# Layer A's attention on one core: two units' outputs in one PSUM bank, and a third bank for late logits

## The chip, the cores and the metric

The kernel runs on one core of one Trainium2 chip. The metric is the device time of one execution in microseconds (us). The kernel before took 2687.64 us, the median of three runs (2687.32, 2687.64 and 2689.79).

## What is computed

Two pre-norm residual layers over 1024 tokens of width 1024. Layer A is sparse attention (16 query heads of 64, one shared key/value head; an indexer picks 256 keys per token) and a squared-ReLU MLP; layer B is latent attention and another MLP. The part that the change touches is layer A's attention, in blocks of 128 queries:

```python
def block(args):                       # one block of 128 queries
    ...
    logits = jnp.einsum('bqhd,bqkd->bhqk', qb, kg) * (A_HEAD_DIM ** -0.5)
    bias = rel_bias[t5_bucket(idx - t[None, :, None])]
    logits = logits + jnp.transpose(bias, (0, 3, 1, 2))
    logits = jnp.where(valid[:, None], logits, NEG)
    p = jax.nn.softmax(logits, axis=-1)
    return jnp.einsum('bhqk,bqkd->bqhd', p, vg)
```

The kernel does not gather the keys: it computes the logits over all admissible keys and adds a mask (`score`, after selection) that is hugely negative at the keys not picked.

## The kernel before

Everything is float32; for speed a matmul operand is split into a high and a low float32r part (`split_evac`, L88: ScalarE casts the high part out of PSUM, VectorE or GpSimd subtracts it to get the low part), and each product is two or three matmuls. A tile framework allocates the buffers, sets every semaphore and orders the instructions of each engine at build time by its own timeline; the source order is a hint. So a change of buffers can move instructions that it does not name.

`attend_a` runs twice: for the early query blocks 1, 3, 0, 2 (up to 512 keys, `wide` = 512; 205 to 350 us of the profile) and, after the first MLP on those blocks, for the late blocks 7, 4, 5, 6 (640 to 1024 keys, `wide` = 1024; 757 to 972 us). A unit is one block and two heads (G = 2), so each call has 32 units, (7,0) to (6,7) in the late one. Three kinds of step are woven, the logits of unit k beside the values of unit k-1:

- `logits` (L543 to L554), per head: TensorE computes `lps`, 128 queries by up to 512 keys, in one PSUM bank (two banks, one after the other, for over 512 keys); VectorE reads it once, adding bias (`bm`) or mask (`score`) and taking the running minimum of the negative, into `lg` in SBUF (L548); ScalarE takes the exponential and the sum (L552), VectorE the reciprocal (L553), GpSimd scales (L554). Six `lg` buffers are there in the late call.
- `values` (L566 to L572), per two key blocks: TensorE transposes the probabilities of both heads into `ppt`; `ph` and `pl` (two SBUF buffers each) are its split; then four matmuls of 256 columns accumulate into `po`, 128 x 256 in PSUM.
- `output` (L580 to L584): ScalarE copies two quarters of `po` to SBUF (`of`, two copies), and VectorE adds them to the other two quarters of `po` and writes `res` (two adds). The second add, L584, is the last reader of `po`.
- `project` (L1066, in `out_proj`): the output projection `pwoa` of a finished block, spread over the next eight units. The late call spreads its first one from block 4 on.

PSUM has eight banks of 512 float32 columns. The early call gets the logits' four banks from its caller (`lp` is given), and has two for `pt` (transposes), one for `po`, one for `pwo`. The late call opens its own pool of logits banks, `bufs=2`, and has three for `pt`, two for `po` (half of each is used), one for `pwo`.

Of the kernel before, what the change touches and what calls it, by code (L numbers as in the profile page):

```python
# [10 lines left out]
F32 = mybir.dt.float32  # L11
# [7 lines left out]
P = 128  # L19
# [23 lines left out]
class Trunk:  # L43
# [433 lines left out]
    def attend_a(self, tbs, res, kh, kl, vv, score, edge, near_d, wst, lp=None, start=None, beside=None, free=None):  # L477
# [4 lines left out]
        H, G = 16, 2  # L482
        wide = (max(tbs) + 1) * P
        nm0 = f"{tbs[0]}"
        with ExitStack() as st:
            qp = st.enter_context(tc.tile_pool(name="atq" + nm0, bufs=2))
            pp = st.enter_context(tc.tile_pool(name="atp" + nm0, bufs=2, space=PSUM))
            lp = lp or st.enter_context(tc.tile_pool(name="atl" + nm0, bufs=2, space=PSUM))
            queries, probs, outs = {}, {}, {}

            def shape(tb):
                S = (tb + 1) * P
                return S, min(S, 256)
# [5 lines left out]
            def cuts(S, far):  # L499
                if S <= 512:  # L500
                    return [(0, S)]
                cut = min(far, 512)
                return [(0, cut), (cut, S)]
# [17 lines left out]

            def logits(tb, g, i):
                S, nr = shape(tb)
                far = S - nr
                mask = edge[:, 256 - S:256] if tb < 2 else score[tb]
                if i == 0:
                    bm = t2.tile([P, G, 256], F32, name=f"bm{tb}_{g}", tag="bm")
                    src = near_d[G * g:G * g + G, 127:127 + P * 383].rearrange("h (t j) -> t h j", j=383)
                    nc.sync.dma_start(bm[:, :, :nr], src[:, :, 256 - nr:256])
                    nc.gpsimd.tensor_tensor(bm[:, :, :nr], bm[:, :, :nr],  # L530
                                            mask[:, far:].unsqueeze(1).to_broadcast([P, G, nr]), op=ALU.add)
                    small = t2.tile([P, 5 * G], F32, name=f"sm{tb}_{g}", tag="sm")
                    probs[tb, g] = (bm, small, [])
                bm, small, ps_h = probs[tb, g]
                hd = G * g + i
                lg = t2.tile([P, wide], F32, name=f"lg{tb}_{hd}", tag="lg", bufs=6 if wide > 512 else 5)
                mf, mg, mn, sm, rs = (small[:, 5 * i + k:5 * i + k + 1] for k in range(5))

                last = 3.0e38
                for b0, b1 in cuts(S, far):  # L540
                    lps = lp.tile([P, 512], F32, name=f"lps{tb}_{hd}_{b0}", tag="pt")
                    for n, kk in enumerate((kh, kl)):
                        nc.tensor.matmul(lps[:, :b1 - b0], queries[tb][1][:, hd, :], kk[:, b0:b1], start=(n == 0), stop=(n == 1))  # L543
                    for c0, c1 in ((b0, min(b1, far)), (max(b0, far), b1)):
                        if c0 < c1:
                            near = c0 >= far
                            least = mn if near else mg if b0 else mf
                            nc.vector.tensor_tensor_reduce(lg[:, c0:c1], lps[:, c0 - b0:c1 - b0],  # L548
                                                           bm[:, i, c0 - far:c1 - far] if near else mask[:, c0:c1], -1.0, last,
                                                           op0=ALU.add, op1=ALU.min, accum_out=least)  # L550
                            last = least
                nc.scalar.activation(lg[:, :S], lg[:, :S], AF.Exp, bias=mn, scale=-1.0, accum_out=sm)  # L552
                nc.vector.reciprocal(rs, sm)  # L553
                nc.gpsimd.tensor_scalar(lg[:, :S], lg[:, :S], rs, 1.0, op0=ALU.mult, op1=ALU.mult)  # L554
                ps_h.append(lg)

            def values(tb, g, s0):
                nb = tb + 1
                if s0 == 0:
                    outs[tb, g] = pp.tile([P, G * P], F32, name=f"po{tb}_{g}", tag="po", bufs=2 if wide > 512 else 1)  # L560
                po, ps_h = outs[tb, g], probs[tb, g][2]
                ns = min(2, nb - s0)
                pt = pp.tile([P, 2, G, P], F32, name=f"ppt{tb}_{g}_{s0}", tag="pt", bufs=3 if wide > 512 else 2)
                for u in range(ns):
                    for i in range(G):
                        self.anchor = nc.tensor.transpose(pt[:, u, i], ps_h[i][:, (s0 + u) * P:(s0 + u + 1) * P], self.ident)  # L566
                ph = t2.tile([P, 2, G * P], F32R, name=f"ph{tb}_{g}_{s0}", tag="ph")
                pl = t2.tile([P, 2, G * P], F32R, name=f"pl{tb}_{g}_{s0}", tag="pl")
                self.split_evac(ph[:, :ns], pl[:, :ns], pt[:, :ns].rearrange("p u a b -> p u (a b)"))
                for u in range(ns):  # L570
                    for n, m in enumerate((ph, pl)):
                        nc.tensor.matmul(po, vv[:, s0 + u], m[:, u], start=(s0 + u == 0 and n == 0),  # L572
                                         stop=(s0 + u == nb - 1 and n == 1))
# [27 lines left out]
            if beside:  # L601
                spread(beside(lambda shape, name: pp.tile(shape, F32, name=name, tag="pwo", bufs=1)), 0, n0)
# [4 lines left out]
            for k in range(NU + 1):  # L607
                if k == n0 + 1:
                    if free:
                        free()  # L610
                    wop = wst.enter_context(tc.tile_pool(name="awo" + nm0, bufs=1, side="right"))
                    wo, load = self.load_wo(wop, t1, self.d["a_w_o"][0], "a" + nm0)
                    spread(load, n0, n1)
                first = [lambda i=i: logits(*units[k], i) for i in range(G)] if k < NU else []
                second, extra = [], []
                if k:
                    tb, g = units[k - 1]
                    second = [lambda s0=s0: values(tb, g, s0) for s0 in range(0, tb + 1, 2)] + [lambda: output(tb, g)]
                    m = (k - 1 - n1) // each
                    if k > n1 and (k - 1 - n1) % each == 0 and m < 3:  # L620
                        spread(project(tbs[m]), k - 1, k - 1 + each)
                    extra = work[k - 1]
                steps = []
                for i in range(max(len(first), len(second))):
                    steps += second[i:i + 1] + first[i:i + 1]
                weave(steps, extra, self.behind)
# [632 lines left out]
```

## Time and profile before

| | |
|---|---|
| median of three runs | 2687.64 us |
| the profiled execution's own time | 2684.85 us |
| its span, first to last instruction | 2683.0 us |
| mean granted TensorE clock | 0.984 |
| TensorE matmul / weight load busy | 94% / 80% |
| VectorE, ScalarE, GpSimd busy | 57%, 46%, 38% |
| early call, late call | some 145 us and 215 us of the span |

The profiled execution lies 2.79 us under the median of the runs. The shares are means over stages with different limits; the two calls of `attend_a` have far busier VectorE than the MLPs, which fill TensorE alone.

### The profile page before, as it was taken

The page shows a single profiled execution, that of the slowest core. Times are in us where ns is not written, and L with a number is a line of the kernel's source. Part 1 is how long each engine was busy: PE and PEld are TensorE (multiplying, and loading weights), DVE is VectorE, ACT ScalarE, POOL GpSimd, SP SyncE. Part 2 cuts the span into 40 slices and gives each one's busy share as a digit, 9 for nine tenths or more (in the row PEclk, how much of TensorE's full clock was granted, in tenths as well). Part 3 has the DMA queues.
Part 4 walks back from the last instruction along what each step waited for, and adds up shares of the span by engine and source line. Part 5 has one row for each costly group of instructions (what it writes and reads, how often), then busy time and mean ns, then how long its engine had stood idle before and what let it go on. Part 6 is the DMA issues. An engine that isn't in the chain of part 4 may idle for free.

```text
span 2683.0 us, 36853 instructions
## 1 busy us (share of the span) xinstructions
PE 2532.4 (94%) x13354; PEld 2148.5 (80%) x13354; DVE 1521.1 (57%) x3655; ACT 1232.2 (46%) x2989; POOL 1024.1 (38%) x756
## 2 busy tenths in 40 slices
PE   6997799999989999999998999998999999999999
PEld 5897678888768888888888788887778888888887
DVE  5798754999869861222257878897422232222223
ACT  4575744333357764243345777787222222222221
POOL 2235635443556535343324555555121212222120
PEclk9998999999999999999999999999999999999999
DMA  7202323222232223233210000002210101111111
GB/s 157 54 24 60 99 92 97 94 99 90 79 110 68 60 82 127 84 120 106 77 33 11 10 14 10 14 5 80 102 32 32 63 32 63 47 48 48 48 47 63
DMA packets 122293, 173.03 MB, mean 64 GB/s; under 512 B 12752, under 2 KB 101104, under 8 KB 122112
## 3 DMA queue, kind: packets, MB, share of 16 engines
q1 hardware_dynamic: 122112, 170.69, 20.5%
q8 instruction: 105, 1.72, 0.3%
q14 instruction: 76, 0.62, 0.1%
HBM read 159.13 MB, written 11.53 MB: 64 GB/s over the span
## 4 chain that ended last, share of the span: by engine, by line
PE 71%; DVE 7%; DMA 3%; ACT 3%; POOL 2%; issue 2%; SPq 0%; POOLq 0%; DVEq 0%; ACTq 0%
PE pd L1190 25%; PE pu L1120 25%; PE pwo L1066 3%; PE pwoa L1066 2%; PE blps L938 2%; PE bpo L962 2%; PE puq L794 2%; PE po L572 1%; PE ppt L566 1%; PE lps L543 1%; PE pcq L853 1%; PE pukv L750 1%; DVE bpr L939 1%; PE bpt L957 1%; PE pck L853 1%
## 5 line engine op out<-in xcount | busy, mean ns | idle before, releaser
L88 POOL TENSOR_TENSOR dl<-rd,dh 128x1024 fp32r<-128x1024 f32 x96 | 232.4, 2429 | 728.2 <-PE pu L1120 369.3
L1191 DVE TENSOR_TENSOR res<-res,pd 128x1024 f32<-128x1024 f32 x192 | 234.2, 1220 | 419.1 <-PE pd L1190 419.1
L1120 PE MATMUL pu<-mxh,uh 128*128 128x512 f32 (+1 forms) x1056 | 405.4, 384 | 2.4 <-DVE mxl L88 2.4
L1120 PE MATMUL pu<-mxl,uh 128*128 128x512 f32 (+1 forms) x1056 | 404.9, 383 | 0.0
L1120 PE MATMUL pu<-mxh,ul 128*128 128x512 f32 (+1 forms) x1056 | 404.9, 383 | 0.0
L1190 PE MATMUL pd<-dh,hh 128*128 128x512 f32 x1024 | 398.6, 390 | 5.1 <-DVE res L1191 3.1
L1190 PE MATMUL pd<-dl,hh 128*128 128x512 f32 x1024 | 398.5, 389 | 0.0
L1190 PE MATMUL pd<-dh,hl 128*128 128x512 f32 x1024 | 392.9, 389 | 1.6 <-DVE hl L88 1.6
L88 DVE TENSOR_TENSOR hl<-pu,hh 128x512 fp32r<-128x512 f32 (+1 forms) x132 | 88.8, 674 | 407.6 <-ACT hh L88 407.6
L88 ACT CAST dh<-rd 128x1024 fp32r<-128x1024 f32 x96 | 99.1, 1051 | 476.1 <-PE pd L1190 422.5
L88 POOL TENSOR_TENSOR ul<-ru,uh 128x1024 fp32r<-128x1024 f32 x96 | 231.9, 2418 | 167.2 <-ACT uh L88 166.9
L1177 ACT ACTIVATE pu<-pu 128x512 f32<-128x512 f32 (+1 forms) x132 | 75.0, 569 | 433.2 <-PE pu L1120 427.7
L1120 PEld LDWEIGHTS pu<-mxh,uh 128*128 128x128 f32 x1056 | 199.1, 189 | 41.7 <-DVE mxl L88 2.9
L1120 PEld LDWEIGHTS pu<-mxl,uh 128*128 128x128 f32 x1056 | 198.9, 188 | 39.0
L1120 PEld LDWEIGHTS pu<-mxh,ul 128*128 128x128 f32 x1056 | 199.0, 188 | 38.7
L1190 PEld LDWEIGHTS pd<-dh,hh 128*128 128x128 f32 x1024 | 192.3, 188 | 46.5 <-DVE res L1191 4.0
L1190 PEld LDWEIGHTS pd<-dh,hl 128*128 128x128 f32 x1024 | 192.2, 188 | 42.1 <-DVE hl L88 2.2
L1190 PEld LDWEIGHTS pd<-dl,hh 128*128 128x128 f32 x1024 | 192.3, 188 | 39.7
L444 DVE TENSOR_SCALAR_CACHE_REDUCE both<-score,cand 128x1024 f32<-128x1024 f32 (+1 forms) x192 | 181.2, 944 | 5.0
L944 POOL TENSOR_SCALAR bpr<-bpr,bsm 128x640 f32<-128x640 f32 (+7 forms) x128 | 98.4, 772 | 96.4 <-DVE bsm L943 55.9
L554 POOL TENSOR_SCALAR lg<-lg,sm 128x256 f32<-128x256 f32 (+7 forms) x128 | 99.4, 783 | 76.7 <-DVE sm L553 54.0
L88 ACT CAST uh<-ru 128x1024 fp32r<-128x1024 f32 x96 | 99.9, 1044 | 30.4 <-DMA ru<-in_mlp_w_up_dram 28.4
(374 smaller groups left out, 5982.0 us busy)
## 6 DMA issues: line engine op xcount, KB each, us to landing
ru<-in_mlp_w_up_dram SPq DMA_DIRECT2D x48, 1024.0 KB, 5.4
rd<-in_mlp_w_down_dram SPq DMA_DIRECT2D x48, 1024.0 KB, 4.9
bm<-near_d SPq DMA_DIRECT2D x56, 256.0 KB, 2.7
res<-in_x_dram SPq DMA_DIRECT2D x16, 512.0 KB, 6.3
wor_a<-in_a_w_o_dram SPq DMA_DIRECT2D x16, 512.0 KB, 3.6
wr_q<-in_a_w_in_dram SPq DMA_DIRECT2D x8, 512.0 KB, 8.7
x<-res SPq DMA_DIRECT2D x8, 512.0 KB, 2.6
wor_b<-in_b_w_o_dram SPq DMA_DIRECT2D x8, 512.0 KB, 3.6
```

Of the source, the lines that this page charges most:

```text
L88: return self.nc.scalar.copy(h, src), (engine or self.nc.vector).tensor_sub(l, src, h)
L444: nc.vector.tensor_scalar(scratch[0][0][:, :s.shape[-1]], s, cand[:, j:j + 1], None, op0=ALU.is_ge, op1=ALU.add, accum_out=cnt[:, j:j + 1])
L554: nc.gpsimd.tensor_scalar(lg[:, :S], lg[:, :S], rs, 1.0, op0=ALU.mult, op1=ALU.mult)
L794: nc.tensor.matmul(ps[:, 192 * u:192 * u + 192], a[:, kb, tsl], b[:, kb], start=(kb == 0 and i == 0), stop=(kb == 2 and i == 2))
L853: nc.tensor.matmul(ps, a[:, kb], b[:, kb], start=(kb == 0 and i == 0), stop=(kb == KB - 1 and i == 2))
L938: nc.tensor.matmul(lps, q[0:rows, tsl], k[0:rows, h, c:c + a], start=(m == 0), stop=(m == 2))
L944: nc.gpsimd.tensor_scalar(pr, pr, sm[:, 3:4], 1.0, op0=ALU.mult, op1=ALU.mult)
L1066: nc.tensor.matmul(open_ps[n], x[:, kb], w[:, kb, ns], start=(kb == 0 and i == 0), stop=(kb == KB - 1 and i == 2))
L1120: nc.tensor.matmul(pu, a[:, kb], b[:, kb, c0:c1], start=(kb == 0 and i == 0), stop=(kb == KB - 1 and i == 2))
L1177: nc.scalar.activation(pu, pu, AF.Relu)
L1190: nc.tensor.matmul(pd[:, ns], a[:, tsl], b[:, ns], start=(f == 0 and k == 0), stop=(f == NS - 1 and k == 2))
L1191: nc.vector.tensor_add(res[:, tb], res[:, tb], pd)
```

## The change

```diff
--- before.py
+++ after.py
@@ -488,6 +488,8 @@
             lp = lp or st.enter_context(tc.tile_pool(name="atl" + nm0, bufs=2, space=PSUM))
             queries, probs, outs = {}, {}, {}
 
+            po_all = pp.tile([P, 2, G * P], F32, name=f"po{nm0}", tag="po", bufs=1)
+
             def shape(tb):
                 S = (tb + 1) * P
                 return S, min(S, 256)
@@ -538,7 +540,7 @@
 
                 last = 3.0e38
                 for b0, b1 in cuts(S, far):
-                    lps = lp.tile([P, 512], F32, name=f"lps{tb}_{hd}_{b0}", tag="pt")
+                    lps = lp.tile([P, 512], F32, name=f"lps{tb}_{hd}_{b0}", tag="pt", bufs=3 if wide > 512 else 4)
                     for n, kk in enumerate((kh, kl)):
                         nc.tensor.matmul(lps[:, :b1 - b0], queries[tb][1][:, hd, :], kk[:, b0:b1], start=(n == 0), stop=(n == 1))
                     for c0, c1 in ((b0, min(b1, far)), (max(b0, far), b1)):
@@ -557,7 +559,7 @@
             def values(tb, g, s0):
                 nb = tb + 1
                 if s0 == 0:
-                    outs[tb, g] = pp.tile([P, G * P], F32, name=f"po{tb}_{g}", tag="po", bufs=2 if wide > 512 else 1)
+                    outs[tb, g] = po_all[:, g % 2]
                 po, ps_h = outs[tb, g], probs[tb, g][2]
                 ns = min(2, nb - s0)
                 pt = pp.tile([P, 2, G, P], F32, name=f"ppt{tb}_{g}_{s0}", tag="pt", bufs=3 if wide > 512 else 2)
```

One tile `po_all` takes a whole bank, allocated at the start of each call. Unit g of a block writes and reads the half g % 2. In the early call that is the one bank that `po` had, now with two halves; in the late call one of the two `po` banks goes, and the logits pool has three banks in place of two. The four banks of logits in the early call are the four that it had. All instructions, operands and DMAs are the same; two lines in, so L572 is now L574, L584 is L586, L543 is L545.

The framework keeps engines apart by bank, not by half. What that makes of the order is shown at three places. In the rows, `[waits ...]` names the engines whose semaphore an instruction waits for.

**TensorE, early call, where unit (1,1) starts its `po`** (`ph1_1_0` is the first split of that unit). Before:

```order
L543 MATMUL lps1_11_0_2716<-kh_73,qst1_2161 128x256 [waits DVE_49]
L543 MATMUL lps1_11_0_2716<-kl_74,qst1_2161 128x256
L572 MATMUL po1_1_2449<-ph1_1_0_2455,vv_75 128x256 [waits DVE_49,PE_49,Activation_49]
L572 MATMUL po1_1_2449<-pl1_1_0_2456,vv_75 128x256
L572 MATMUL po1_1_2449<-ph1_1_0_2455,vv_75 128x256
L572 MATMUL po1_1_2449<-pl1_1_0_2456,vv_75 128x256
```

With the change:

```order
L545 MATMUL lps1_11_0_2712<-kh_73,qst1_2162 128x256 [waits DVE_49]
L545 MATMUL lps1_11_0_2712<-kl_74,qst1_2162 128x256
L574 MATMUL po1_1996<-ph1_1_0_2454,vv_75 128x256 [waits DVE_49,Activation_49]
L574 MATMUL po1_1996<-pl1_1_0_2455,vv_75 128x256
L574 MATMUL po1_1996<-ph1_1_0_2454,vv_75 128x256
L574 MATMUL po1_1996<-pl1_1_0_2455,vv_75 128x256
```

Nothing moved, and the first matmul of the unit waits for VectorE and ScalarE as before: in the built program for the second `res` add and the second `of` copy of unit (1,0), though these read the other half. This holds for all units of the early call, and on every engine the order is the same up to the late call (from the first instruction to row 3668 of TensorE's 13353 matmuls).

**TensorE and VectorE, late call, between units (7,1) and (7,2).** Before, on TensorE (`po_1_...` is unit (7,1)'s output, `po_2_...` that of (7,2), `ppt_2_...` transposes of (7,2)):

```order
L543 MATMUL lps_9_0_7382<-kh,qst_6995 128x512 [waits DVE_49,PE_49]
L543 MATMUL lps_9_0_7382<-kl,qst_6995 128x512
L572 MATMUL po_2_7245<-ph_2_0_7251,vv 128x256 [waits Activation_49]
L572 MATMUL po_1_7153<-pl_1_6_7229,vv 128x256 [waits DVE_49]
L572 MATMUL po_1_7153<-ph_1_6_7228,vv 128x256
L572 MATMUL po_1_7153<-pl_1_6_7229,vv 128x256
L566 MATMUL ppt_2_4_7302<-ident,lg_4_7171 128x128
L566 MATMUL ppt_2_4_7302<-ident,lg_5_7197 128x128
L566 MATMUL ppt_2_4_7302<-ident,lg_4_7171 128x128
L566 MATMUL ppt_2_4_7302<-ident,lg_5_7197 128x128
L572 MATMUL po_2_7245<-pl_2_0_7252,vv 128x256 [waits DVE_49]
L572 MATMUL po_2_7245<-ph_2_0_7251,vv 128x256
```

With the change, all outputs are in `po_6961`; the last `po` matmul of (7,1) stands one row above the first row shown:

```order
L568 MATMUL ppt_2_4_7269<-ident,lg_5_7165 128x128
L568 MATMUL ppt_2_4_7269<-ident,lg_4_7139 128x128
L568 MATMUL ppt_2_4_7269<-ident,lg_5_7165 128x128
L568 MATMUL ppt_2_6_7282<-ident,lg_4_7139 128x128 [waits DVE_49]
L568 MATMUL ppt_2_6_7282<-ident,lg_5_7165 128x128
L568 MATMUL ppt_2_6_7282<-ident,lg_4_7139 128x128
L568 MATMUL ppt_2_6_7282<-ident,lg_5_7165 128x128
L568 MATMUL ppt_3_0_7304<-ident,lg_6_7230 128x128 [waits DVE_49,Pool_49]
L568 MATMUL ppt_3_0_7304<-ident,lg_7_7256 128x128 [waits Pool_49]
L568 MATMUL ppt_3_0_7304<-ident,lg_6_7230 128x128
L568 MATMUL ppt_3_0_7304<-ident,lg_7_7256 128x128
L574 MATMUL po_6961<-ph_2_0_7218,vv 128x256 [waits DVE_49,Activation_49]
```

Before, (7,2) starts its `po` in the middle of (7,1)'s last four matmuls; now all of (7,1)'s come first, then twelve transposes, then the first `po` of (7,2), which waits for the second `res` add of (7,1) on VectorE and the copies on ScalarE. On VectorE before:

```order
L88 TENSOR_TENSOR pl7_1_6_7229<-ppt7_1_6_7223,ph7_1_6_7228 128x512
L88 TENSOR_TENSOR pl7_2_0_7252<-ppt7_2_0_7246,ph7_2_0_7251 128x512
L548 ISA lg7_8_7355,sm7_4_7354<-lps7_8_512_7360,score7_82,sm7_4_7354 128x256
L548 ISA sm7_4_7354 128x1
L548 ISA lg7_9_7381,sm7_4_7354<-lps7_9_0_7382,score7_82 128x512
L548 ISA sm7_4_7354 128x1
L553 RECIPROCAL sm7_3_7262<-sm7_3_7262 128x1
L548 ISA lg7_8_7355,sm7_4_7354<-lps7_8_512_7360,bm7_4_7351,sm7_4_7354 128x256
L548 ISA sm7_4_7354 128x1
L88 TENSOR_TENSOR pl7_2_2_7282<-ppt7_2_2_7276,ph7_2_2_7281 128x512
L583 TENSOR_TENSOR res_69<-po7_1_7153,of7_1_7236 64x128
L584 TENSOR_TENSOR res_69<-po7_1_7153,of7_1_7236 64x128
```

and with the change:

```order
L88 TENSOR_TENSOR pl7_1_4_7184<-ppt7_1_4_7178,ph7_1_4_7183 128x512
L550 ISA lg7_9_7347,sm7_4_7320<-lps7_9_512_7352,bm7_4_7317,sm7_4_7320 128x256
L550 ISA sm7_4_7320 128x1
L88 TENSOR_TENSOR pl7_1_6_7197<-ppt7_1_6_7191,ph7_1_6_7196 128x512
L555 RECIPROCAL sm7_4_7320<-sm7_4_7320 128x1 x2
L88 TENSOR_TENSOR pl7_2_0_7219<-ppt7_2_0_7213,ph7_2_0_7218 128x512
L88 TENSOR_TENSOR pl7_2_2_7249<-ppt7_2_2_7243,ph7_2_2_7248 128x512
L585 TENSOR_TENSOR res_69<-po7_6961,of7_1_7204 64x128
L586 TENSOR_TENSOR res_69<-po7_6961,of7_1_7204 64x128
L550 ISA lg7_10_7412,sm7_5_7411<-lps7_10_0_7413,score7_82 128x512
```

Ahead of the two `res` adds VectorE now has both `pl` of (7,2) and two reciprocals, and the logits of head 10 and 11 behind them, where it had those of heads 8 and 9 ahead: the logits run further ahead of the values. All 31 boundaries of the late call have this form; between the last `po` matmul of a unit and the first of the next stand 12 to 26 other matmuls.

**TensorE, start of the late call.** Before:

```order
L543 MATMUL lps_0_0_7031<-kh,qst_6995 128x512
L543 MATMUL lps_0_0_7031<-kl,qst_6995 128x512
L543 MATMUL lps_0_512_7035<-kh,qst_6995 128x512
L543 MATMUL lps_0_512_7035<-kl,qst_6995 128x512
L543 MATMUL lps_1_0_7044<-kh,qst_6995 128x512 [waits DVE_49]
L543 MATMUL lps_1_0_7044<-kl,qst_6995 128x512
L543 MATMUL lps_1_512_7048<-kh,qst_6995 128x512 [waits DVE_49,PE_49]
L543 MATMUL lps_1_512_7048<-kl,qst_6995 128x512
L543 MATMUL lps_2_0_7080<-kh,qst_6995 128x512 [waits DVE_49]
```

With the change:

```order
L545 MATMUL lps_0_0_7001<-kh,qst_6965 128x512
L545 MATMUL lps_0_0_7001<-kl,qst_6965 128x512
L545 MATMUL lps_0_512_7005<-kh,qst_6965 128x512
L545 MATMUL lps_0_512_7005<-kl,qst_6965 128x512
L545 MATMUL lps_1_0_7014<-kh,qst_6965 128x512
L545 MATMUL lps_1_0_7014<-kl,qst_6965 128x512
L545 MATMUL lps_1_512_7018<-kh,qst_6965 128x512 [waits DVE_49]
L545 MATMUL lps_1_512_7018<-kl,qst_6965 128x512
L545 MATMUL lps_2_0_7049<-kh,qst_6965 128x512 [waits DVE_49]
```

The third pair of logits matmuls (`lps_1_0`) has a bank of its own and waits for nothing; the later pairs wait for a read one bank further back.

In layer B's attention, which the change does not name, the framework's order also comes out differently in many places, with the same instructions.

## Rows read from the trace of the kernel before

**Rows 1.** Early call: busy time of each engine, granted clock, DMA.

```profile
core 0: us, PE busy (x) PEld busy (x) DVE busy (x) ACT busy (x) POOL busy (x), PEclk, DMA share, GB/s
205.00:345.00 140.00, 107.64 (x677) 92.55 (x675) 109.63 (x410) 90.85 (x268) 90.53 (x102) 0.89 0.29 84
```

**Rows 2.** Tile `of`, both calls: who waited for it, us, times.

```profile
  PEld po L572: 1.5, 1
...
  PE po L572: 1.3, 1
```

**Rows 3.** Late call, five stages, columns as in Rows 1.

```profile
757.00:776.00 19.00, 13.67 (x59) 9.46 (x58) 12.17 (x35) 10.29 (x15) 12.63 (x9) 0.82 0.45 141
776.00:831.00 55.00, 48.80 (x338) 42.22 (x338) 51.03 (x159) 45.76 (x89) 43.28 (x32) 1.00 0.30 87
831.00:872.00 41.00, 40.12 (x280) 36.95 (x279) 37.11 (x114) 30.27 (x72) 21.35 (x21) 1.00 0.21 59
872.00:922.00 50.00, 48.53 (x324) 43.08 (x324) 44.01 (x137) 36.43 (x77) 26.84 (x25) 1.00 0.19 54
922.00:972.00 50.00, 47.42 (x314) 42.21 (x312) 43.08 (x139) 34.90 (x76) 20.56 (x19) 1.00 0.13 38
```

**Rows 4.** Late call, VectorE's waits: us in total, times, longest.

```profile
DVE sm L553 <- ACT lg L552: 5.2, 10, 1.3
DVE pl L88 <- ACT ph L88: 4.5, 13, 0.7
DVE lg L548 <- PE lps L543: 4.3, 11, 0.7
DVE res L1191 <- PE pd L1190: 4.2, 1, 4.2
```

**Rows 5.** Late call, TensorE's waits, the same columns.

```profile
PE lps L543 <- DVE sm L548: 4.5, 7, 2.4
...
PE po L572 <- DVE pl L88: 3.7, 5, 2.7
```

**Rows 6.** Timeline of VectorE: start, us, instruction [idle before <-releaser].

```profile
767.59 0.48 DVE L548 CUSTOM_DVE_ANT_0 lg<-lps,score,sm 128x256 f32<-128x256 f32 x1 [0.28 <-PE lps L543]
...
769.99 0.48 DVE L548 CUSTOM_DVE_ANT_0 lg<-lps,score,sm 128x256 f32<-128x256 f32 x1 [0.69 <-PE lps L543]
```

**Rows 7.** Timeline: end of unit (4,1), start of (4,2).

```profile
841.71 0.28 PE L572 MATMUL po<-pl,vv 128*128 128x256 f32 x1
...
842.29 0.26 ACT L580 COPY of<-po 64x128 f32<-64x128 f32 x1
...
843.10 0.28 PE L572 MATMUL po<-ph,vv 128*128 128x256 f32 x1
...
843.35 0.29 DVE L584 TENSOR_TENSOR res<-po,of 64x128 f32<-64x128 f32 x1
```

**Rows 8.** Timeline: last `po` matmul and L584, units (7,0), (6,6).

```profile
782.05 0.29 PE L572 MATMUL po<-pl,vv 128*128 128x256 f32 x1
...
784.19 0.29 DVE L584 TENSOR_TENSOR res<-po,of 64x128 f32<-64x128 f32 x1
...
966.72 0.28 PE L572 MATMUL po<-pl,vv 128*128 128x256 f32 x1
...
968.00 0.29 DVE L584 TENSOR_TENSOR res<-po,of 64x128 f32<-64x128 f32 x1
```

**Rows 9.** Chain of work in order of time: start, us, what.

```profile
805.30 0.47 PE po L572 x4
...
805.88 0.46 PE lps L543 x2
...
828.25 0.44 PE ppt L566 x4
...
842.21 0.70 PE pwoa L1066 x3
```

**Rows 10.** Layer B's attention: what TensorE waits for longest.

```profile
PE bpo L962 <- DVE bpl L88: 10.9, 19, 1.6
```

## The prediction, made before the changed kernel had run

> **What bounds the kernel now.** First the page's shares (TensorE 94%, VectorE 57%): as means they say that TensorE is the bound and that nothing else matters. The change touches two stages alone, so the table by windows comes next, and there the mean is wrong. In the early call TensorE is busy for 107.6 of 140 us and VectorE for 109.6 [rows 1]: neither is full, both wait for each other. In the late call the reader sees three regimes [rows 3]. At the start (757 to 776) both idle. In block 7 (776 to 831) VectorE is busy for 51.0 of 55 us and TensorE for 48.8: VectorE sets the pace, as a unit of block 7 brings it four `pl` splits and six reads of logits. From block 4 on, when the output projection is woven in, TensorE is busy for 40.1 of 41, 48.5 of 50 and 47.4 of 50 us, and VectorE for 37.1, 44.0 and 43.1: TensorE sets the pace, with VectorE close behind. Then the table of waits: VectorE waits 4.3 us in the late call for a pair of logits matmuls [rows 4], TensorE 4.5 us for VectorE to empty a logits bank [rows 5]; these are largely the same stalls, seen from both sides. No row has a wait of `po` for the two adds in the late call, since there two banks are there.
>
> **The change part by part.**
>
> *Early call: nothing.* The order is the same on all engines, and the first matmul of each unit waits for the two adds and the copies of the unit before, as it did with one buffer. The second half is a buffer by its address, not by its waits. If it were a real one, it could take away what `po` waits for the output step at present, at most 1.5 us [rows 2]. I take 0; the ends are -1.5 and 0.
>
> Those rows show how little is there, not why halves would not do. The Trainium skill (PSUM — Partial Sum Buffer, section "PSUM bank collisions raise a hardware error") gives a reason that speaks against this change: two engines may not touch the same bank in the same 32 partitions at once, whatever the columns, and the hardware neither arbitrates nor stalls, so software must keep them apart by bank. By that rule the early sum is 0 for any order; without it, it would be the -1.5 us above. The order's waits agree with the rule; no run here shows a collision.
>
> *Late call, the third bank of logits: a gain.* At the start the third pair of logits matmuls loses its wait, and later pairs wait for a read one bank further back. VectorE's waits for logits, 4.3 us in 11 pieces, are what this can remove; the rows at 767.59 and 769.99, 0.28 and 0.69 us, are such pieces [rows 6]. In blocks 4 to 6, where TensorE sets the pace, removing one is worth nothing. I take half, -2.0 us; the ends are -4.3 and 0. TensorE's 4.5 us are not added to it. The third bank leaves its other cover in place: six `lg` buffers still stop the logits from running further.
>
> *Late call, one `po` bank in place of two: a new wait.* It stands at all 31 boundaries between units, on the first `po` matmul of a unit, and behind it in TensorE's queue wait that unit's other `po` matmuls, the transposes of its later key blocks, the next logits and the projection. What it waits for is a chain: last `po` matmul, two copies on ScalarE, two adds on VectorE, each behind what stands ahead in its queue. From the start of the last matmul to the end of the second add the chain took 1.93 us at unit (4,1), 841.71 to 843.64, with the next unit's first `po` already at 843.10 [rows 7]; 2.43 us at the first boundary and 1.57 at the last of the 31 [rows 8]. Read off in the same way at all of them, the median is 2.1 us, four are over 3, the longest is 4.7.
>
> Against it stands what TensorE does meanwhile. Its paces are 0.11 us for a transpose, 0.12 for a `po` matmul, 0.46 for a pair of 512-column logits and 0.70 for three projection matmuls [rows 9]. By the changed order there are 1.4 to 2.9 us of other work at the boundaries of block 7 (12 transposes, 1.3 us, and the last `po` itself at the shortest), 2.1 to 4.4 in blocks 4 and 5, where the projection's 1.4 us a unit help, and 1.9 to 2.8 in block 6. Boundary by boundary, chain less cover, where positive: 6.4 us in block 7, 2.3 in block 4, 0.3 in block 5, 1.2 in block 6, together 10.2.
>
> Which of it counts? In block 7 VectorE is the bound, and when TensorE halts there, up to three filled banks of logits are ready for VectorE: three reads of 0.48 us [rows 6] or more cover most halts. So the 6.4 us are worth 0 as long as VectorE has work. From block 4 on a halt counts in full, but the 2.3 us of block 4 come from two long chains; at (4,0) a split of the projection's operand stood ahead of the adds on VectorE, and the changed order no longer has it there. That leaves 1.5 us. I take +1.5; the ends are 0 and +10.2.
>
> *Layer B's attention, reordered.* No buffer changes there. Its longest wait is 10.9 us in 19 pieces [rows 10]; that a different order moves a fifth of this either way, 2 us, is an estimate from that row. I take 0, from -2 to +2. The MLPs, which are most of the span, keep their order and are filled by TensorE.
>
> **Sum.** 0 - 2.0 + 1.5 + 0 = -0.5 us. Against the profiled execution's 2684.85 us that is 2684.35. That execution lies 2.79 us under the median of the runs; I carry the difference, not the level: 2687.64 - 0.5 = **2687.1 us**. About 0.2%, 5.4 us, is what a measurement of this kernel can tell from no change.
>
> **The rivals.**
>
> *Slower: the new wait closes a loop.* `ph` and `pl` have two buffers each. The third split of a unit needs the first one's buffer, which comes free with the unit's first `po` matmuls, which now wait for the adds of the unit before. So adds, first `po`, third split, later `po`, copies and adds again form a loop through TensorE, ScalarE and VectorE that the second bank had cut. Its price is the whole shortfall, 10.2 us, block 7's part included: 2697.8 us. For it: VectorE and TensorE are both within a tenth of full, and both `pl` of the next unit stand ahead of the adds. Against it: the order was rebuilt around the wait, with more work between the units. It decides when VectorE, in block 7, has read its three banks before the halt ends; a halt of over 1.5 us can do that.
>
> *Faster: VectorE runs through.* The order has the logits up to a unit further ahead. Then the waits for the exponential (5.2 us) and for `ph` (4.5 us) [rows 4] shrink together with the 4.3. The most that block 7 and the start can give is VectorE's idle time there, 74 - 63.2 = 10.8 us [rows 3], less the 4.2 us that it waits for the MLP's last matmuls [rows 4]: 6.6 us, so 2681.0 us. For it: VectorE is the bound in just that stretch. Against it: it must lose nearly all its gaps, and none of it may be given back from block 4 on.
>
> *The change does nothing that can be seen.* The halves are no buffers, the third bank fills the same gaps that `lg` and VectorE's pace leave open: then layer B's order alone is left, 2687.6 us within 2. It lies inside my forecast.
>
> **How the numbers follow.** Forecast, within 0.2%, 0.53, of which some 0.15 is that nothing is seen; its own range is -4.3 - 1.0 to +3.8 + 1.0, 2682.3 to 2692.4 (the third bank's best case or blocks 4 to 6's full shortfall, and half of layer B's). Slower, the loop: 0.23, as VectorE and TensorE are both near full and 10.2 us stand at stake. Faster, VectorE through: 0.24, a smaller stake, but where the bound is. The range for 8 in 10 reaches from the faster rival's 2681.0 to nearly all of the slower one's price: 2680.5 to 2697.0. Chances: faster 0.24, same 0.53, slower 0.23.
>
> **What would show it.** In the changed profile the early call's window keeps its busy times within 1 us. From the last matmul of the MLP to the last add, the late call's 213 us stay within 4. A wait of `po` for the adds appears among TensorE's waits: under 4 us from block 4 on if I am right, and around 10 in all with VectorE's waits grown if the loop is. VectorE's wait for logits falls from 4.3 to some 2 us; with 6 us more of VectorE's idle time gone from 757 to 831, the faster rival is right. Layer B's attention keeps its 440 us within 2. The forecast is wrong if the late call changes by over 5 us, or if a stage that I costed at nothing, the early call or layer B, moves by more than 2.

## The result, and the profile after

The changed kernel takes **2704.33 us** (median of 4 runs, 2703.07 to 2707.20) against 2687.48 of the kernel before beside it: ratio 1.0065, 95% interval 1.0052 to 1.0077. It is slower by some 17 us; 2687.1 was forecast, and the range ended at 2697.0. The profiled execution after took 2705.34 us, its span is 2703.6.

The windows of the changed kernel, with the columns of [rows 1]; the late call's five stages are cut where the units of a block end, as in [rows 3]:

```profile
205.00:345.00 140.00, 111.35 (x668) 95.00 (x666) 108.79 (x406) 90.12 (x262) 89.59 (x102) 0.85 0.29 85
...
760.00:779.00 19.00, 14.12 (x65) 9.12 (x64) 13.01 (x42) 10.97 (x16) 13.57 (x10) 0.91 0.44 139
779.00:840.00 61.00, 54.02 (x341) 45.82 (x341) 50.55 (x158) 46.67 (x92) 43.98 (x34) 0.92 0.27 83
840.00:887.00 47.00, 45.05 (x281) 36.95 (x281) 38.70 (x121) 29.60 (x69) 21.81 (x22) 1.00 0.18 51
887.00:944.00 57.00, 52.83 (x324) 42.73 (x323) 44.82 (x139) 35.85 (x79) 25.10 (x24) 1.00 0.17 47
944.00:996.00 52.00, 48.36 (x300) 39.46 (x298) 39.55 (x123) 31.54 (x71) 17.23 (x16) 1.00 0.11 31
```

The five stages took 19, 55, 41, 50 and 50 us before and take 19, 61, 47, 57 and 52 now. VectorE's busy time has not grown: the sum over the five is 186.6 us, 187.4 before [rows 3]. It idles 22 us more. TensorE's longer busy time is no new work: it runs as many matmuls as before (13354 in the span), and their ends are modelled.

The extent of the late call by tile, first and last start in us, of the kernel before:

```profile
L515 PE MATMUL ptq<-identr,qt x64: 220/248/305, 760.5 to 904.1; 128*128 128x128 f32 x64
L572 PE MATMUL po<-pl,vv x208: 274/282/390, 777.5 to 970.8; 128*128 128x256 f32 x104
```

and of the changed one:

```profile
L517 PE MATMUL ptq<-identr,qt x64: 221/248/282, 762.7 to 922.5; 128*128 128x128 f32 x64
L574 PE MATMUL po<-pl,vv x208: 274/281/579, 778.6 to 995.5; 128*128 128x256 f32 x104
```

From the first query transpose to the last `po` matmul the **late call** takes 232.8 us, where it took 210.3: +22.5. This length is called "late call" below. VectorE's waits in it, after (757 to 998):

```profile
DVE sm L555 <- ACT lg L554: 17.5, 30, 1.0
DVE pl L88 <- ACT ph L88: 13.4, 26, 1.6
...
DVE lg L550 <- PE ppt L568: 5.5, 10, 1.0
...
DVE lg L550 <- PE lps L545: 1.0, 2, 0.8
```

The wait for logits fell as forecast, 4.3 to 1.0 us. But the reciprocal's wait for the exponential rose from 5.2 to 17.5 and the split's wait for ScalarE from 4.5 to 13.4 [rows 4]: +21.2 together, nearly the late call's +22.5. The line with `ppt` is new: ten reads of logits waited for transposes, 5.5 us in all, which by the program a read does only to get a free `lg` buffer. TensorE's waits in the same stretch:

```profile
PE po L574 <- DVE pl L88: 6.6, 11, 2.0
PE lps L545 <- DVE sm L550: 3.6, 6, 0.8
...
PE po L574 <- DVE res L586: 0.3, 1, 0.3
```

ScalarE's waits for `po`, before (757 to 975) and after (757 to 998):

```profile
ACT ph L88 <- PE po L572: 26.6, 39, 1.5
```

```profile
ACT ph L88 <- PE po L574: 34.9, 24, 2.7
```

The wait on which the prediction turned, `po` for the two adds, is there once in 31 boundaries, with 0.3 us. What VectorE does in that time is seen in its timeline, one unit of block 4, before (start, us, instruction [idle before <-releaser]; rows that read back accumulators left out):

```profile
838.91 0.29 DVE L584 TENSOR_TENSOR res<-po,of 64x128 f32<-64x128 f32 x1
...
839.43 0.48 DVE L548 CUSTOM_DVE_ANT_0 lg<-lps,bm,sm 128x256 f32<-128x256 f32 x1
...
840.18 0.55 DVE L548 CUSTOM_DVE_ANT_0 lg<-lps,score 128x384 f32<-128x384 f32 x1
...
840.98 0.16 DVE L553 RECIPROCAL sm<-sm 128x1 f32<-128x1 f32 x1 [0.24 <-ACT lg L552]
841.45 0.69 DVE L88 TENSOR_TENSOR pl<-ppt,ph 128x512 fp32r<-128x512 f32 x1 [0.31 <-ACT ph L88]
842.06 0.47 DVE L548 CUSTOM_DVE_ANT_0 lg<-lps,bm,sm 128x256 f32<-128x256 f32 x1
...
843.35 0.29 DVE L584 TENSOR_TENSOR res<-po,of 64x128 f32<-64x128 f32 x1
```

The same of the changed kernel:

```profile
845.47 0.55 DVE L550 CUSTOM_DVE_ANT_0 lg<-lps,score 128x384 f32<-128x384 f32 x1
...
845.95 0.55 DVE L550 CUSTOM_DVE_ANT_0 lg<-lps,score 128x384 f32<-128x384 f32 x1
...
847.31 0.29 DVE L586 TENSOR_TENSOR res<-po,of 64x128 f32<-64x128 f32 x1
847.64 0.48 DVE L550 CUSTOM_DVE_ANT_0 lg<-lps,bm,sm 128x256 f32<-128x256 f32 x1
...
848.05 0.48 DVE L550 CUSTOM_DVE_ANT_0 lg<-lps,bm,sm 128x256 f32<-128x256 f32 x1
...
849.18 0.16 DVE L555 RECIPROCAL sm<-sm 128x1 f32<-128x1 f32 x1 [0.65 <-ACT lg L554]
850.00 0.16 DVE L555 RECIPROCAL sm<-sm 128x1 f32<-128x1 f32 x1 [0.65 <-ACT lg L554]
850.25 1.17 DVE L88 TENSOR_TENSOR pl<-ppt,ph 128x256 fp32r<-128x256 f32 x2
...
853.22 0.29 DVE L586 TENSOR_TENSOR res<-po,of 64x128 f32<-64x128 f32 x1
```

and its ScalarE at that time:

```profile
848.23 0.83 ACT L554 ACTIVATE lg<-lg,sm 128x640 f32<-128x640 f32 x1 [2.35 <-DVE sm L550]
...
849.06 0.81 ACT L554 ACTIVATE lg<-lg,sm 128x640 f32<-128x640 f32 x1
```

A block 4 head's logits are read in two parts, the first with `score`, the second with `bm`; only then can its exponential start. Before, the reads are strung head by head, with other work between a head's last read and its reciprocal. Now VectorE reads first part, first part, second part, second part of a unit's **two heads in a pair**. ScalarE idles 2.35 us until the first head's second part is read, which now stands behind the other head's first part, a split and the two adds. Then it runs two exponentials back to back, and the reciprocals behind them hold VectorE 0.65 us each; the next splits stand behind both. From add to add a unit takes 5.9 us (847.31 to 853.22); before it took 4.4 (838.91 to 843.35).

In the new order, another read stands between the first and the last read of a head for all 64 heads of the late call; before for 20, 9 of them in block 7 and 11 in block 6, none in blocks 4 and 5. The sharp form shown here, two second parts with nothing but the read-back of an accumulator between them, is in 15 of the changed kernel's 32 units (2, 4, 5 and 4 in blocks 7, 4, 5 and 6), and in none before. On TensorE a head's two logits pairs follow each other in both.

Outside the late call: the early call's busy times on TensorE and VectorE are 111.4 and 108.8 us (107.6 and 109.6 before [rows 1]). Layer B, from its first logits to its last `bpo`, after:

```profile
L940 PE MATMUL blps<-kth,qth x192: 223/415/637, 1473.9 to 1875.8; 104*128 104x384 f32 x48, 104*128 104x512 f32 x48, 104*128 104x320 f32 x32, 104*128 104x448 f32 x32
...
L964 PE MATMUL bpo<-bpl,bv x192: 219/400/776, 1493.1 to 1906.9; 128*128 128x512 f32 x96, 128*128 128x384 f32 x32, 128*128 128x256 f32 x32, 128*128 128x128 f32 x32
```

That is 433.0 us; before it was 438.1 in the profiled execution. The experiments below give 432 to 435, also e1, whose trace shows the order of the kernel before there on every engine (434.2). Whether a part of these 5 us comes from the change stays open; the experiments speak for scatter of the one execution that there is of before.

### The profile page after: what moved, and what is told of

Read it like the earlier page. It is cut to its first block, busy times and chain, and to the rows that moved or that the text cites. A ratio compares the mean times of both kernels' runs of the same rounds, so it can differ in the third digit from the quotient of the medians.

```text
span 2703.6 us, 36892 instructions
## 1 busy us (share of the span) xinstructions
PE 2554.4 (94%) x13354; PEld 2152.1 (80%) x13354; DVE 1517.1 (56%) x3655; ACT 1229.2 (45%) x2989; POOL 1020.5 (38%) x756
## 4 chain that ended last, share of the span: by engine, by line
PE 53%; DVE 4%; ACT 2%; DMA 1%; POOL 1%; issue 1%; SPq 0%; DVEq 0%; ACTq 0%; POOLq 0%
PE pu L1122 19%; PE pd L1192 19%; PE pwo L1068 3%; PE blps L940 2%; PE puq L796 2%; PE bpo L964 1%; DVE bpr L941 1%; PE pukv L752 1%; PE pcq L855 1%; PE bpt L959 1%; PE pck L855 1%; DMA ukr<-in_w_ukv_dram 1%; DVE bpl L88 1%; ACT bpr L944 0%; DMA uqr<-in_b_w_uq_dram 0%
## 5 line engine op out<-in xcount | busy, mean ns | idle before, releaser
L554 ACT ACTIVATE lg<-lg,sm 128x256 f32<-128x256 f32 (+7 forms) x128 | 99.0, 775 | 41.5 <-DVE sm L550 39.6
```

## The experiments

All kernels at a glance. "Paired" counts the late call's heads (of 64) with another read between their first and last read on VectorE, by the order; "late call us" is read from one profiled execution; the time is a median, and the ratio is to the kernel before run beside it, with the 95% interval.

| kernel | output banks | logits banks | split buffers | paired | late call us | time us | ratio |
|---|---|---|---|---|---|---|---|
| before | 2 | 2 | 2 | 20 | 210.3 | 2687.48 | 1 |
| changed | 1 | 3 | 2 | 64 | 232.8 | 2704.33 | 1.0065 [1.0052, 1.0077] |
| e1 | 1 | 2 | 2 | 13 | 219.2 | 2693.38 | 1.0023 [1.0010, 1.0036] |
| e2 (one `ppt` bank less) | 2 | 3 | 2 | 60 | 232.8 | 2706.84 | 1.0077 [1.0062, 1.0092] |
| e3 | 1 | 3 | 4 | 40 | 207.7 | 2683.03 | 0.9991 [0.9979, 1.0002] |
| e4 | 2 | 2 | 4 | 13 | 216.8 | 2691.14 | 1.0018 [1.0009, 1.0028] |
| e5 | 1 | 3 | 2 | 2 | 220.4 | 2692.90 | 1.0023 [1.0014, 1.0033] |
| e6 | 2 | 2 | 2 | 64 | 217.8 | 2692.04 | 1.0021 [1.0012, 1.0031] |
| e7 | 1 | 3 | 4 | 12 | 205.2 | 2676.16 | 0.9960 [0.9948, 0.9973] |
| e8 | 1, undivided | 3 | 2 | 64 | 230.4 | 2703.13 | 1.0061 [1.0041, 1.0081] |
| e9 (adds first) | 1 | 3 | 2 | 2 | 238.7 | 2707.71 | 1.0078 [1.0063, 1.0093] |
| e10 | 1 | 2 | 4 | 14 | 213.3 | 2686.71 | 0.9997 [0.9987, 1.0006] |
| e11 | 2 | 2 | 4 | 10 | 214.3 | 2685.12 | 0.9996 [0.9986, 1.0005] |
| e12 (adds off VectorE) | 1 | 3 | 4 | 6 | 202.6 | 2679.55 | 0.9972 [0.9963, 0.9981] |

**First round: loop or look-ahead.** Theory A was the slower rival (the one bank closes a loop through the two split buffers), theory B that the third logits bank lets the logits run too far ahead of the values.

e1, the change with two logits banks (one bank left empty):

```
-  ... tag="pt", bufs=3 if wide > 512 else 4)   # lps
+  ... tag="pt", bufs=2 if wide > 512 else 4)
```

> The change without its third logits bank: outputs of two units in one bank, two banks of logits as before, one bank left empty. From the last add of the MLP ahead of it to the last output add, the late call took 213 us before and 236 us with the change. Theory A (loop): the single output bank makes a unit's first output matmuls wait for the adds of the unit before, and these hold up the third split of the unit. Then this kernel is about as slow as the change: late call 232 to 242 us, total 2700 to 2712 us. Theory B (look-ahead): the third logits bank lets the framework put logits ahead of the values, and VectorE and ScalarE come late to the splits. Then this one is close to the kernel before: late call 213 to 219 us, total 2686 to 2694 us.

e2, the kernel before with three logits banks, for which `ppt` and `ptq` give one up:

```
-  ... tag="pt")                                # lps
+  ... tag="pt", bufs=3 if wide > 512 else 4)
-  ... tag="pt", bufs=3 if wide > 512 else 2)   # ppt, ptq
+  ... tag="pt", bufs=2)
```

> The kernel before with the third logits bank alone; the bank comes from the transposes, which have two in place of three, and the outputs keep two banks. Theory A: the output wait is absent, so late call at most 220 us (the lost transpose bank costs something, the third logits bank gives at most 4 us), total under 2695 us. Theory B: slow like the change, late call 230 us or more, total over 2700 us.

e3, the change with four `ph` and `pl` buffers in the late call, and e4, the kernel before with the same:

```
-  ph = t2.tile(..., tag="ph")
+  ph = t2.tile(..., tag="ph", bufs=4 if wide > 512 else 2)   # pl likewise
```

> The change, with four buffers each for the high and the low split of the probabilities in the late call, in place of two. The output bank and its wait stay. Theory A: all splits of a unit can be done ahead of its output matmuls, the loop is cut, and most of the loss comes back: late call 213 to 222 us, total 2684 to 2696 us. Theory B: the splits do not wait for buffers but for their place in the order; late call 230 us or more, total over 2699 us.

> Control for the run above: the kernel before with four split buffers each. Theory A: with two output banks the loop is already cut, so little is to be had, late call 208 to 214 us, total 2681 to 2690 us. Theory B has nothing to say against that. If it gains as much as the change regains with the same edit, the split buffers were short in both and that run tells nothing on the output bank.

Neither theory stood by itself. e1 cost 6.6 us (2693.38 against 2686.79 beside it), two fifths of the loss: far under A's figure and at the upper edge of B's. e3 lost nothing with the third bank in place, against B. e2 is slow, but one `ppt` bank less could be why: ScalarE's `ph` waits 43.8 us for `ppt` there. And e4 was slower than the kernel before, though it only has more buffers. The framework lays out the late call anew whenever a buffer count changes, so each kernel also had an **order** of its own. That gave theory C: the pairing in VectorE's queue.

**Second round: the order alone.** e5 is the change, its buffers untouched, with an edge (an order that the framework has to keep) that makes VectorE read a unit's second head behind its first:

```
+  if wide > 512 and i and hd - 1 in done_at:
+      behind.enter_context(self.tc.issue_after(done_at[hd - 1].ins))
-  nc.vector.tensor_tensor_reduce(lg[:, c0:c1], ...
+  done_at[hd] = nc.vector.tensor_tensor_reduce(lg[:, c0:c1], ...
```

> The change as it is, with one edit: in the late call VectorE may not take the second head of a unit's logits before the first head's are complete. Theory C (pairing: with three banks of logits the framework lists, on VectorE, the first parts of both heads before the second part of either, in 64 of 64 heads against 20 of 64 before; each first head's exponential starts a logits operation later, both exponentials run back to back and the two reciprocals behind them hold VectorE): late call from 232.8 to 210-222 us, total 2682-2696, VectorE's waits of sm for ScalarE's lg from 17.5 to under 9 us. Theory A (loop through the one bank of outputs and the two split buffers): both stay as they are in the change, so 2700-2708. Theory B (logits too far ahead because of the third bank): the third bank stays, 2698-2708.

e6 is the kernel before, made to read in pairs: the second part of a unit's first head is written behind the second head's first part, with such an edge.

```
+  if i == 0:
+      rest = products(*parts[1])
+      held[0] = lambda behind: (take(rest, *parts[1], behind), weights())
+  else:
+      held[0](state[1])
+      take(products(*parts[1]), *parts[1])
+      weights()
```

> The kernel before, its two output banks and two logits banks kept, with VectorE made to take a unit's logits in the change's order (first part of one head, first part of the other, then the second parts). Theory C: late call from 210.3 to 215-228 us, total 2691-2705. Theories A and B: nothing of the buffers changes, 2684-2690.

e7 is e3 with e5's edge:

> The change with four split buffers (which came to 2683.03, late call 207.7 us, 40 of 64 heads paired) and, besides, VectorE kept to one head after the other. Theory C: the pairs left cost some, so 2676-2683, late call 200-207. Theory A: the loop is open in both, so the same within 2 us, 2681-2686. If pairing helps where the splits are free: 2684-2692.

e8 replaces the shared bank by one output buffer that is not divided:

```
-  outs[tb, g] = po_all[:, g % 2]
+  outs[tb, g] = pp.tile([P, G * P], F32, name=f"po{tb}_{g}", tag="po", bufs=1)
```

> One output buffer of one unit that is not divided, in place of a bank shared by two units, and three banks of logits: the order on every engine is that of the change. All theories: as the change, 2700-2708, since the halves decouple nothing. If the two halves let one unit's outputs be written while the other's are read: slower than the change, 2710-2725.

VectorE's waits in the late call of e5 (758 to 985):

```profile
DVE pl L88 <- ACT ph L88: 10.6, 21, 1.5
DVE sm L563 <- ACT lg L562: 6.8, 20, 0.6
```

Theory C held in e5. With no buffer changed its median is 11.4 us under the change's (2692.90 against 2704.33). The two ran beside different runs of the kernel before: against those the loss falls from 16.9 to 6.7 us, by 10.2, and so it does against e8, which ran beside e5 (2703.13). The late call is 12.4 us shorter than the change's, 10.0 shorter than e8's, and the reciprocal's wait falls from 17.5 to 6.8 us. The edge moved more than the pairs: over 100 of the late call's some 1310 TensorE matmuls stand at another place. So e5 shows what the order is worth at equal buffers; that it is the pairing within the order rests on the waits.

e6, with no buffer changed either, is 5.8 us slower than before (2692.04 against 2686.25). That is inside theory C's range, but no more than what order alone moves between e4 and e11, two kernels with 13 and 10 paired heads (6.0 us). The blocks tell more. Here are their lengths in us, from the first query transpose to the last `po<-pl` matmul of each block in turn, and the units whose two second parts follow each other directly:

| kernel | block 7 | block 4 | block 5 | block 6 | such units, of 32 |
|---|---|---|---|---|---|
| before | 70.3 | 41.3 | 50.0 | 48.7 | 0 |
| changed | 75.7 | 48.8 | 56.6 | 51.7 | 15 |
| e8 | 73.4 | 48.8 | 56.6 | 51.6 | 15 |
| e5 | 71.5 | 45.5 | 51.0 | 52.3 | 0 |
| e6 | 73.8 | 42.5 | 48.8 | 52.7 | 0 |

In blocks 4 and 5 e6 takes the logits of all 16 units as the change does, first, first, second, second part, and loses nothing (91.3 us, as before), where the change loses 14. It loses in blocks 7 and 6. Its second parts never follow each other directly. In the unit shown, a split stands between them:

```profile
847.46 0.48 DVE L557 CUSTOM_DVE_ANT_0 lg<-lps,bm,sm 128x256 f32<-128x256 f32 x1
...
847.87 0.69 DVE L88 TENSOR_TENSOR pl<-ppt,ph 128x512 fp32r<-128x512 f32 x1
...
850.08 0.48 DVE L557 CUSTOM_DVE_ANT_0 lg<-lps,bm,sm 128x256 f32<-128x256 f32 x1
```

so the two exponentials do not queue up there. In blocks 4 and 5 the pairs as such then cost nothing. What sets the change apart is the form with both second parts back to back and the splits behind both reciprocals: only the change, e8 and e2 (19 units) have it, and with e9 they are the slowest four. No run made that form alone.

e8 has the order of the change on TensorE, VectorE and ScalarE and takes its time: the two halves of the bank decouple nothing. e7 is the fastest of all, at 0.9960. Its late call by windows, and VectorE's waits in it (758 to 985):

```profile
760.00:966.00 206.00, 193.95 (x1296) 170.57 (x1296) 183.30 (x578) 156.18 (x325) 124.84 (x104) 0.98 0.24 70
```

```profile
DVE pl L88 <- ACT ph L88: 6.1, 11, 1.2
...
DVE sm L563 <- ACT lg L562: 4.4, 6, 1.1
...
DVE lg L557 <- PE lps L549: 1.4, 4, 0.6
```

**Third round: what is left, and what pays.** e9 is e5 with a unit's two adds ahead of the next unit's first split on VectorE:

```
+  if wide > 512 and s0 == 0 and 'out' in done_at:
+      behind.enter_context(self.tc.issue_after(done_at['out'].ins))
   nc.vector.tensor_sub(pl[:, :ns], ..., ph[:, :ns])
```

> The change with heads apart (2692.9, late call 220.4) and, besides, VectorE made to take a unit's two output adds ahead of the next unit's first split, so that the one bank is free before the next unit's splits fill the two split buffers. Theory A for what is left over the kernel before (the loop through the bank and the split buffers): ScalarE's wait of ph for TensorE's po falls from 36 to under 25 us, late call 208-215, total 2681-2688. Theory D (the loss left is the wait for the last products of a unit itself, which VectorE now takes earlier in its queue): the splits behind the adds come later, late call 220-230, total 2692-2704.

e10 is e7 with two logits banks, e11 is e4 with e5's edge:

> The fastest version so far (change, four split buffers, heads apart: 2676.16, late call 205.2) with two banks of logits in place of three; one bank is left empty. If the third logits bank is what pays once pairing and the loop are away: 2682-2692, late call 211-221, VectorE waits again for lps (1.4 us with three, 4.3 before). If the four split buffers and the order do it all: 2674-2679.

> The kernel before, its two output banks and two logits banks kept, with four split buffers and heads apart: the fastest version without the change. If the third logits bank is what pays: 2685-2692, as the kernel before with four split buffers (2691.14). If split buffers and order do it all, the second output bank can only help: 2670-2677.

e12 is e7 with the output's adds taken off VectorE in the late call:

```
+  if wide > 512:
+      nc.scalar.copy(dst[0:64], po[0:64, 0:P])
+      nc.scalar.copy(dst[64:128], po[64:128, P:2 * P])
+      nc.gpsimd.tensor_tensor(dst, dst, of, op=ALU.add)
+      return
```

> The fastest version so far (change, four split buffers, heads apart: 2676.16, late call 205.2 us, VectorE busy 183 and ScalarE 156 of 206) with the late call's output taken off VectorE: ScalarE copies all four quarters out of the bank and GpSimd adds them in SBUF. If VectorE's own work is what bounds the late call now: VectorE gives up 32 units' two adds, some 0.57 us each, 18 us busy; late call 192-203, total 2663-2674. If ScalarE's queue is what VectorE waits for: 32 times two more copies of some 0.3 us in it, late call 205-215, total 2676-2687.

e9 missed theory A's numbers and went beyond theory D's. ScalarE's waits in it (758 to 1000):

```profile
ACT ph L579 <- DVE pl L583: 26.7, 21, 2.1
ACT ph L579 <- PE po L586: 22.2, 29, 2.3
```

The wait for `po` fell from 36.2 (e5) to 22.2, as A asked, but the splits now stand behind the adds and ScalarE waits for them instead; VectorE waits 14.4 us for the copies `of`. Freeing the bank by moving the adds up only moved the halt.

e10 tells what the third logits bank is worth: with one output bank, four split buffers and heads apart, two logits banks give a ratio of 0.9997 and three (e7) 0.9960, some 10 us of 2687. The two have nearly as many paired heads (14 and 12), though each has its own order. Without the change at all (e11) it is 0.9996. So by these runs e7's gain needs the change's third bank **and** the split buffers.

e12 takes 16 us of busy time off VectorE:

```profile
760.00:966.00 206.00, 194.84 (x1297) 170.76 (x1298) 167.25 (x517) 171.84 (x391) 136.32 (x136) 0.98 0.24 70
```

and is not faster than e7: 0.9972 against 0.9960, intervals overlapping. Its time lies in the range that was given to ScalarE's queue; its late call, 202.6 us against 205.2 in one profile each, in that of VectorE's work. VectorE's wait for `ph` rises from 6.1 to 14.9 us. So work taken off VectorE did not shorten the whole; that the hand-overs between ScalarE and VectorE are the bound is the likely reading, and no run shows it.

## Why the prediction was wrong

- **Early call, 0: right, by the experiments.** VectorE's busy time in the window is 0.8 us down, but TensorE's is 3.7 up, where 1 was allowed, at a granted clock of 0.85 (0.89 before); e8, without halves, shows the same, 111.9 us at 0.84. From its first `ptq` to its last `po` the call took 176.6 us in the changed kernel and 174.6 before, but 175.7 and 175.9 in e4 and e6, where it is as before, and 175.5 to 176.5 in e5, e7 and e8. e8 shows why nothing came of it: halves are no buffers. This agrees with the Trainium skill (PSUM — Partial Sum Buffer, section "PSUM bank collisions raise a hardware error"), which has software guard a bank, not an address; no run here shows a collision.
- **The third logits bank, -2.0, from -4.3 to 0: this step failed, by its sign.** The wait it was to remove did go (4.3 to 1.0 us). But I excluded a loss with the sentence that the third bank "leaves its other cover in place", and counted only what a bank more lets TensorE do. It also let the framework put VectorE's reads in pairs. With the same buffers and the pairs taken out by an edge, some 10 of the 17 us came back (e5). The cover it named, the six `lg` buffers, did stop the logits, and VectorE stood still for it, 5.5 us. With few pairs or none the third bank is worth nothing beside two split buffers (e5 and e1 both 1.0023, each in its own order). The Trainium skill (Perfetto Trace Analysis, section "Matmul Optimizations") asks that all eight PSUM banks be used. Here e1, which leaves one empty, beats the change by some 10 us; with four split buffers the runs agree with that rule (e7 over e10).
- **One output bank, +1.5, from 0 to +10.2: inside its ends, mis-sized.** e1 has that term alone, in an order of its own: +6.6 us. With the 10.2 from e5 that makes 16.8 against 16.9 measured, which says only that e1 and e5 came out alike: the 10.2 is the whole loss less e5's.
- **How it costs: not as the step had it.** I looked for TensorE's halt at the first `po` of a unit. It is one row of 0.3 us. The cost appears on ScalarE, whose `ph` waits for `po` (26.6 us before, 34.9 after, 28.7 in e1), and on VectorE behind it, whose splits wait for `ph` (4.5 before, 13.4 after, 9.6 in e1). That is the direction of the slower rival, whose loop runs through the two split buffers. With four of them one output bank costs nothing clear of noise (e10 0.9997, e11 0.9996) in place of 6.6 us, as the loop would have it. It is not settled: each of these kernels has its own order, and e4 against e11, which differ in the edge alone, shows that order by itself moves 6.0 us with hardly any pairs. A run of one and two output banks under one order was not made.
- **Where: the wrong stages.** The forecast costed block 7 at 0 as VectorE would have "up to three filled banks of logits" to read, and let only TensorE's halts count from block 4 on. VectorE hardly waited for a bank (1.0 us); it could not reach them: reciprocals and splits that waited for ScalarE stood ahead of them in its queue. Blocks 7, 4, 5 and 6 lost 6, 6, 7 and 2 us by the windows; some 2 of block 7's are the clock's (last section). Most went in blocks 4 and 5, to which the forecast gave 2.6 us of halts on TensorE. Nor was there anything for the third bank to win in block 7: VectorE's eleven waits for logits before [rows 4] lie at 762 to 773 and from 849 us on, and none falls together with one of TensorE's [rows 5], so they are not "the same stalls, seen from both sides". The sum did not add the two.
- **Layer B, 0 within 2:** 5 us shorter in the one profile of each, and open, as said above.
- **The rivals.** The slower one had the right side; its price, 10.2 us, is three fifths of what was measured, and the output bank on which it rests came to 6.6 alone (e1). The faster one, by which the waits for the exponential and for `ph` "shrink together", had it the wrong way round: these are the two waits that grew. e7 goes below the time it named (2681.0), with the wait for logits at 1.4 us and those two at 4.4 and 6.1, before 5.2 and 4.5.

The rows to read were at hand. The order of VectorE between (7,1) and (7,2) showed two reciprocals back to back (x2) with no logits between them and the splits. I read it as "logits further ahead"; [rows 4] had the price of a reciprocal's wait, 5.2 us for 10, and the question was how often the new order would make VectorE wait for ScalarE.

## What to carry to other kernels

Where a framework lays out the queues, a change of a buffer count is also a change of order: read the new order on the engine that paces the stage for each instruction that waits for another engine (here reciprocal and split), and ask how much work stands between its input's start and its place. A buffer more need not pay when what it feeds is held by a shorter buffer further on: here the third bank was worth 0 with two split buffers and some 10 us with four, each kernel in its own order. To tell buffers from order, pin the order with an edge and keep the buffers, as e5 and e6 do. Then look at the result stage by stage: e6's total seemed to bear out the pairing, while its blocks 4 and 5, with the pairs as in the change, had lost nothing.

## What the runs showed of the hardware that was not expected

The granted clock in the block 7 window of the changed kernel's profile was 0.92, a mean over stretches at 2.4 and at 1.2 GHz (1.00 before). e8, with the same order, was granted 1.00 in the same window:

```profile
779.00:840.00 61.00, 52.45 (x351) 42.91 (x351) 52.08 (x166) 47.47 (x93) 44.32 (x33) 1.00 0.28 83
```

It got further in these 61 us: TensorE did 351 matmuls against 341, VectorE 166 instructions against 158. By the table of blocks, block 7 took 75.7 us in the changed kernel and 73.4 in e8, and blocks 4, 5 and 6 took the same in both within 0.1. So even in this stage, where TensorE waits for other engines, the lower clock goes with 2.3 us more. That is one execution of each, but all else in the late call agrees. Of the 22.5 us that the late call grew in the profile, some 2 are then the clock's, and 20 the change's.
